# Float32 probabilities with 128-wide values in differential attention, a column-packed condition product, and moved splits in the MLP

## The chip, the cores and the metric

One core of a Trainium2 chip runs the whole program. The metric is the device time of one execution in microseconds, lower is better. The engines are TensorE (PE, with its weight loads listed apart as PEld), VectorE (DVE), ScalarE (ACT), GpSimd (POOL) and SyncE (SP), which issues most of the DMAs. Each engine works through its own instructions in order and waits on semaphores.

## The reference

Two blocks follow each other on 1024 tokens of width 1024. The first block has two layers with 256 context tokens; each layer has three kinds of attention, and the first kind, differential attention, is the one that the change touches. The second block mixes three other heads and ends in an MLP with a squared ReLU. Cut to what matters here:

```python
# the condition: shift, scale and gate from silu(c) @ w_ada + b_ada, for c and for c_ctx
# first kind of attention: 4 heads, two maps of width 32, values of width 64
def diff_attend(q, k, v, lam):
    s = jnp.einsum('bqhmd,bkhmd->bhmqk', q, k).astype(jnp.float32) * (q.shape[-1] ** -0.5)
    p = jax.nn.softmax(s, axis=-1)
    a = (p[:, :, 0] - lam * p[:, :, 1]).astype(v.dtype)
    return jnp.einsum('bhqk,bkhd->bqhd', a, v)

# the end of the second block: width 1024 -> 4096 -> 1024
h = h + jnp.square(jax.nn.relu(hn @ w_up[l])) @ w_down[l]
```

## The kernel before

**Precision.** Most large products are float32 products in three passes: each operand is split into a high part in the reduced float32 type (a ScalarE copy) and a low part (a subtraction on VectorE or GpSimd), and `mm3` (lines 73 to 75) adds high times high, high times low and low times high. A few products take plain float32 operands. A plain float32 product appears in the trace as two TensorE instructions, one in the reduced type as one.

**The condition.** `ada_first` (lines 101 to 127) multiplies `silu(c)` (two columns: c and c_ctx) with the first 2048 columns of `w_ada`, 8 pieces of 1 MB through four buffers, 4 products of 512 columns for each piece, all plain float32. Two rows of the result are transposed by 16 small transposes (line 126). `modulate` makes from them the shift and gain that the first tile of the first projection needs.

**Attention.** `attend_kind` treats a kind as a row of units, one unit for each head and 128 queries (and one for both context tiles, in layer 0). The order of the work on every engine is written out by hand in `cfgs[...]["order"]`: S scores, M row minimum, E exponential, C combination of the two maps, T transposes, K copies out of PSUM, J pieces of the product with v, O1 to O4 output. The kinds run in the order A, C, B in both layers. For kind A the probabilities of one unit are 128 x 1280, transposed in three groups of 4, 4 and 2 blocks. `whole=4` means that the first four blocks of 128 keys are split: ScalarE copies the group out of PSUM (`pf`, line 728), GpSimd makes the high part (`th`, line 729) and the low part (`tl`, line 730). The other six blocks stay float32 (`tf`, line 724). `products` then works for each pair of units: four blocks give two products each (high and low) against `v`, which holds the two parts of the values beside each other, 128 wide; six blocks give one float32 product each against `vf`, the sum of both parts, 64 wide, made by GpSimd once for each head (line 425) after the load of v. `cuts` says at which products the six J pieces begin. `load_head` issues the loads of the next head on GpSimd's queue, four for k and q and one for v, when the current head is at its third unit.

**The MLP.** Both MLP products use a seven-product scheme over 2 x 2 blocks, with numbers p from 1 to 7. `mlp_up` runs 16 column groups g; `prep` makes the parts `wh` and `wl` of a weight (lines 1589, 1571), two steps ahead; `wl` goes to VectorE for the first six steps and for p of 1 or 2, otherwise to GpSimd. `startup` makes the split right-hand factors B[1] to B[7] during the first steps; the low part of B[4] is made on GpSimd, and only when it is done is the space of `hraw` free, on which the tiles of `late` lie. `mlp_down` runs 4 slices s with seven products each; its own `prep` splits a weight tile `w` (VectorE) and an activation tile `u` (GpSimd), two halves each (lines 1742 and 1710). The first of these preparations stands behind the last step of `mlp_up`. In the last slice the finished sums are combined (line 1711) and stored.

## Time and profile before

| | |
|---|---|
| median of 3 runs | 3794.61 us (3781.96 to 3800.78) |
| the profiled execution | 3782.26 us |
| its span, first to last instruction | 3780.5 us |
| TensorE busy | 3441.1 us (91%) |
| VectorE busy | 2397.9 us (63%) |
| ScalarE busy | 1763.5 us (47%) |
| GpSimd busy | 1594.2 us (42%) |
| mean granted TensorE clock | 0.957 of full speed |

The stages lie in the span as follows: the condition from 0 to 43 us, the projection of layer 0 to 495 us, kind A to about 700, C to about 890, B to about 1085, the output product to 1160; in layer 1 the projection to about 1620, kind A to about 1830, C to 1995, B to 2215, the output product to 2300; then the second block with its projections, its scans from about 2700, its output product, the first MLP product from 3127 to 3451 and the second to the end.

A busy share is an average over these stages. In a table of stretches the columns are: the stretch, its length, for each engine its busy time and number of instructions, the granted clock as a share of full speed, the busy share of the DMA engines and GB/s. In a list of instructions in order of time the columns are: start, duration, engine, line, operation, what it writes and reads, how many were merged, and in brackets the idle time of the engine before it and what ended it. Records of TensorE overlap (the end contains the way through the array), so its pace is read from start to start.

### The profile page before, as it was taken

What the parts mean: (1) busy time and instruction counts of PE and PEld (TensorE: products, weight loads), DVE (VectorE), ACT (ScalarE), POOL (GpSimd) and SP (SyncE); (2) the same over time, 40 slices, a digit from 0 to 9 for tenths busy, and PEclk for the clock granted to TensorE, in tenths of its full rate; (3) what the DMA queues carried; (4) which work ended last, traced back from release to release, by engine and by line L of the source; (5) the groups of instructions that cost most, each with busy time, mean ns of one, the idle gap of its engine ahead of it and who ended that gap; (6) DMA issues with size and microseconds to landing.
All of it is one profiled execution on the core that took longest, in us unless ns stands there. A gap on an engine that the chain in (4) does not pass through costs nothing. (4 is left out here: it accounts for less than half of the span.)

```text
span 3780.5 us, 50490 instructions
## 1 busy us (share of the span) xinstructions
PE 3441.1 (91%) x17986; PEld 2760.7 (73%) x17986; DVE 2397.9 (63%) x4543; ACT 1763.5 (47%) x3667; POOL 1594.2 (42%) x1692
## 2 busy tenths in 40 slices
PE   8989978888989899978898989999799898999999
PEld 5767755677877788756677767887677677887887
DVE  5666469777774635559776664422688637555778
ACT  4212257677851422247667733321476525554432
POOL 1146434325760235535426741112455415554556
PEclk9999989999999999979999989999899999999999
DMA  7564662662223434592661124121311223545542
GB/s 264 194 182 131 152 111 48 95 115 51 43 79 131 166 126 143 140 113 45 108 100 42 23 104 162 60 64 51 89 40 37 76 84 126 164 153 188 194 144 106
DMA packets 281359, 420.20 MB, mean 111 GB/s; under 512 B 49586, under 2 KB 179186, under 8 KB 276370
## 3 DMA queue, kind: packets, MB, share of 16 engines
q1 hardware_dynamic: 204244, 336.07, 27.4%
q0 software_dynamic: 76864, 80.90, 14.1%
q8 instruction: 142, 2.33, 0.3%
q14 instruction: 109, 0.89, 0.1%
HBM read 289.30 MB, written 127.48 MB: 110 GB/s over the span
## 5 line engine op out<-in xcount | busy, mean ns | idle before, releaser
L74 PE MATMUL mm<-wlo,hh 128*128 128x512 f32 (+2 forms) x1400 | 546.0, 390 | 18.1 <-POOL wlo L94 11.7
L73 PE MATMUL mm<-whi,hh 128*128 128x512 f32 (+2 forms) x1400 | 553.5, 396 | 8.8 <-ACT hh L68 5.3
L75 PE MATMUL mm<-whi,hl 128*128 128x512 f32 (+2 forms) x1400 | 546.7, 391 | 2.1 <-DVE hl L69 2.1
L698 PE MATMUL T<-ident,p 128*128 128x128 f32 x2288 | 382.4, 288 | 37.6 <-DVE y L777 9.5
L94 POOL TENSOR_TENSOR wlo<-wraw,whi 128x512 fp32r<-128x512 f32 (+1 forms) x108 | 164.7, 1532 | 477.6 <-ACT whi L92 402.7
L698 PEld LDWEIGHTS T<-ident,p 128*128 128x128 f32 x2288 | 267.6, 146 | 108.4 <-issue 24.2
L473 PE MATMUL s<-k,q 128*128 128x256 f32 (+2 forms) x904 | 251.0, 384 | 77.9 <-ACT p L476 43.5
L74 PEld LDWEIGHTS mm<-wlo,hh 128*128 128x128 f32 (+1 forms) x1400 | 264.5, 189 | 76.5 <-POOL wlo L94 16.7
L73 PEld LDWEIGHTS mm<-whi,hh 128*128 128x128 f32 (+1 forms) x1400 | 264.5, 189 | 62.6 <-ACT hh L68 6.8
L75 PEld LDWEIGHTS mm<-whi,hl 128*128 128x128 f32 (+1 forms) x1400 | 264.1, 189 | 61.7 <-DVE hl L69 6.0
L730 POOL TENSOR_TENSOR tl<-pf,th 128x512 fp32r<-128x512 f32 (+1 forms) x256 | 288.5, 1133 | 13.4
L729 POOL TENSOR_SCALAR th<-pf 128x512 fp32r<-128x512 f32 (+1 forms) x256 | 153.8, 605 | 267.6 <-ACT pf L728 267.1
L473 PEld LDWEIGHTS s<-k,q 128*128 128x128 f32 x904 | 149.1, 200 | 122.9 <-ACT p L476 66.1
L626 DVE TENSOR_REDUCE mm<-s 128x1 f32<-128x1280 f32 x128 | 188.8, 1477 | 63.8 <-PE s L473 63.5
L69 DVE TENSOR_TENSOR tl<-T,th 128x512 fp32r<-128x512 f32 (+2 forms) x336 | 178.4, 551 | 46.9 <-ACT th L68 44.7
L1710 POOL TENSOR_TENSOR f<-u,f 128x1024 fp32r<-128x1024 f32 x54 | 153.8, 2872 | 121.3 <-issue 106.6
L476 ACT ACTIVATE p<-s,mm 128x1280 f32<-128x1280 f32 (+1 forms) x156 | 184.1, 1183 | 35.8 <-DVE mm L626 32.9
L74 PE MATMUL D<-f,f 128*128 128x512 f32 x448 | 177.2, 396 | 6.0 <-DVE f L1710 5.9
L73 PE MATMUL D<-f,f 128*128 128x512 f32 x448 | 176.7, 395 | 5.6 <-ACT f L1742 5.6
L236 ACT ACTIVATE q_sq<-mm 128x512 f32<-128x512 f32 (+1 forms) x76 | 41.1, 541 | 299.2 <-DVE qk_ss L242 119.1
L73 PE MATMUL mm<-whi,yh 128*128 128x512 f32 x416 | 171.6, 413 | 9.0 <-ACT yh L68 7.3
L94 DVE TENSOR_TENSOR wlo<-wraw,whi 128x512 fp32r<-128x512 f32 (+1 forms) x108 | 102.7, 957 | 120.2 <-ACT whi L92 115.4
(453 smaller groups left out, 9112.3 us busy)
## 6 DMA issues: line engine op xcount, KB each, us to landing
wraw<-in_w_in_dram SPq DMA_DIRECT2D x72, 512.0 KB, 4.2
u<-ud SPq DMA_DIRECT2D x27, 1024.0 KB, 4.8
w<-in_w_adat_dram SPq DMA_DIRECT2D x64, 256.0 KB, 3.3
upraw<-in_w_up_dram SPq DMA_DIRECT2D x32, 512.0 KB, 4.5
ud<-d SPq DMA_DIRECT2D x64, 256.0 KB, 2.6
wq<-in_w_down_dram SPq DMA_DIRECT2D x16, 1024.0 KB, 7.4
v<-vd POOLq DMA_DIRECT2D x24, 640.0 KB, 11.2
q<-qd POOLq DMA_DIRECT2D x24, 640.0 KB, 20.5
```

What stands on the lines that cost most here:

```text
L69: self.nc.vector.tensor_tensor(out=lo, in0=src, in1=hi, op=ALU.subtract)
L73: nc.tensor.matmul(ps, lh, rh, start=first, stop=False)
L74: nc.tensor.matmul(ps, lh, rl, start=False, stop=False)
L75: nc.tensor.matmul(ps, ll, rh, start=False, stop=last)
L94: e.tensor_tensor(out=lo[:, k, :], in0=raw[:, k, :], in1=hi[:, k, :], op=ALU.subtract)
L473: self.nc.tensor.matmul(out, q[:, tcol : tcol + P], ks, start=i == 0, stop=i == len(qs) - 1)
L476: self.nc.scalar.activation(out, in_, AF.Exp, bias=nm, scale=-1.0, accum_out=acc)
L626: nc.vector.tensor_reduce(out=mm[:, m, 0:1], in_=s[:, :SK], axis=AX.X, op=ALU.min)
L698: nc.tensor.transpose(pt[:, i, :], p[:, (4 * g + i) * P : (4 * g + i + 1) * P], self.ident)
L729: nc.gpsimd.tensor_scalar(out=h_, in0=pf, scalar1=1.0, scalar2=0.0, op0=ALU.mult, op1=ALU.add)
L730: nc.gpsimd.tensor_tensor(out=l_, in0=pf, in1=h_, op=ALU.subtract)
L1710: sub = lambda e, o, x, y: e.tensor_tensor(out=o, in0=x, in1=y, op=ALU.subtract)
```

## The change

It has four parts.

1. **Kind A.** `whole` goes from 4 to 0: all ten blocks of the transposed probabilities are copied out of PSUM by ScalarE as float32, no block is split, and GpSimd has neither `th` nor `tl` to make in this kind. `vf` becomes 128 wide, with zeros in columns 64 to 127 (a GpSimd memset for each head), and each pair of units has ten float32 products with 128-wide weights. The cuts of the six J pieces move with it.
2. **The condition.** `silu(c)` is padded to 32 columns, and the four products of a piece write to four groups of 32 columns of the array and 32 rows of PSUM each. The bias row becomes 128 x 2048 with zeros below the first two rows. The 16 transposes become 16 float32 products with a selector that adds the four groups.
3. **First MLP product.** `wl` goes to VectorE for the first twelve steps rather than six. The last column group has the order of the others.
4. **From the first to the second MLP product, and the last slice.** The tiles of B[1] and B[2] are kept and serve as one of two sets of split tiles in `mlp_down` (before: eight rotating tiles). The split of the first pair of factors (`down_split`) is put into `mlp_up`, behind step p = 7 of the last group. In the last slice the additions into A(6) (at p = 1) and A(5) (at p = 7) go from VectorE to GpSimd, those into A(6) one step later.

```diff
@@ ada_first
-            sc = self.t(p, [P, KO, 2], tag="silu_c")
-            nc.sync.dma_start(sc, I["cc"])
...
+            sc = self.t(p, [P, KO, 32], tag="silu_c")
+            nc.vector.memset(sc, 0.0)
+            nc.sync.dma_start(sc[:, :, 0:2], I["cc"])
...
+            row = self.t(p, [P, 4 * 512], tag="row")
+            nc.vector.memset(row, 0.0)
+            nc.sync.dma_start(row[0:2, :], I["b_ada"].broadcast_to([2, 4 * 512]))
+            sel = self.t(p, [P, 2], tag="sel")
...
-                        nc.tensor.matmul(pr, sc[:, kk, :], w[:, k, :], start=kk == 0, stop=kk == KO - 1)
+                        nc.tensor.matmul(pr[32 * k : 32 * k + 32, :], sc[:, kk, :], w[:, k, :], start=hf == 0, stop=hf == 1, tile_position=(0, 32 * k), skip_group_check=True)
...
-                nc.tensor.transpose(pt[:, j, :], row[:, j * P : (j + 1) * P], self.ident[0:2, 0:2])
+                nc.tensor.matmul(pt[:, j, :], row[:, j * P : (j + 1) * P], sel, start=True, stop=True)
@@ load_v
-            vf = self.t(pool, [P, NTA, 64], tag="vf")
+            vf = self.t(pool, [P, NTA, P], tag="vf")
             f = v.bitcast(F32)
-            nc.gpsimd.tensor_tensor(out=vf, in0=f[:, :, 0:64], in1=f[:, :, 64:128], op=ALU.add)
+            nc.gpsimd.memset(vf[:, :, 64:128], 0.0)
+            nc.gpsimd.tensor_tensor(out=vf[:, :, 0:64], in0=f[:, :, 0:64], in1=f[:, :, 64:128], op=ALU.add)
@@ cfgs
-        "A": dict(whole=4, poolg=((0,),), dsplit=SK, pp=6, apl=3, psT=2, psO=0, cuts=(0, 6, 9, 10, 11, 13, 14), order=(
+        "A": dict(whole=0, poolg=((),), dsplit=SK, pp=6, apl=3, psT=2, psO=0, cuts=(0, 2, 4, 6, 7, 9, 10), order=(
@@ products
-                if s >= whole:
-                    ops.append((64, c, w, d["vf"][:, b, :], tf[:, s - whole, c : c + w]))
+                if tf is not None and s >= whole:
+                    ops.append((P, c, w, d["vf"][:, b, :], tf[:, s - whole, c : c + w]))
@@ mlp_first, mlp_up
-        self.bp = self.bs.enter_context(tc.tile_pool(name="mb1", bufs=1, side="right", reuse_waits="tile"))
+        self.bp = self.b1s.enter_context(tc.tile_pool(name="mb1", bufs=1, side="right", reuse_waits="tile"))
-            sub(nc.vector if n < 6 or p in (1, 2) else nc.gpsimd, lo, src, hi)
+            sub(nc.vector if n < 12 or p in (1, 2) else nc.gpsimd, lo, src, hi)
-        steps = first + [(g, p) for g in range(NG) for p in ((1, 6, 2, 5, 7, 3, 4) if g < NG - 1 else (1, 2, 6, 5, 7, 3, 4)) if (g, p) not in first]
+        steps = first + [(g, p) for g in range(NG) for p in (1, 6, 2, 5, 7, 3, 4) if (g, p) not in first]
+            if (g, p) == (NG - 1, 7):
+                self.down_split(self.first[0], self.first[2], [*B[1], *B[2]])
+    def down_split(self, w, u, dst):
+        nc = self.nc
+        wh, wl, uh, ul = dst
+        for k in (0, 2):
+            c = slice(k, k + 2)
+            for hi, lo, x, e in ((wh, wl, w, nc.vector), (uh, ul, u, nc.gpsimd)):
+                nc.scalar.copy(hi[:, c, :], x[:, c, :])
+                e.tensor_tensor(out=lo[:, c, :], in0=x[:, c, :], in1=hi[:, c, :], op=ALU.subtract)
@@ mlp_down
-            hl = E("dhl", 8, side="right")
+            hl = E("dhl", 1, side="right")
+            sets = [[*self.B[1], *self.B[2]], [self.t(hl, [P, 4, 512], F32R, tag=f"f{i}") for i in range(4)]]
...
+                fac[s, p] = sets[(7 * s + order.index(p)) % 2]
+                if (s, p) != (0, 1):
+                    self.down_split(w, u, fac[s, p])
...
-                        add(v, A(6), A(6), a)
                     elif p == 2:
+                        add(gp, A(6), A(6), A(1))
...
-                        add(v, A(5), A(5), a)
+                        add(gp, A(5), A(5), a)
```

## Rows read from the trace of the kernel before

**Rows 1.** The page, part 1: busy time, share of the span, instructions of each engine.
```profile
PE 3441.1 (91%) x17986; PEld 2760.7 (73%) x17986; DVE 2397.9 (63%) x4543; ACT 1763.5 (47%) x3667; POOL 1594.2 (42%) x1692
```
**Rows 2.** Table of stretches: layer 1's kind A, then two of the MLP.
```profile
1720.00:1800.00 80.00, 72.36 (x407) 51.13 (x405) 78.17 (x117) 65.03 (x123) 44.77 (x40) 1.00 0.30 52
...
3440.00:3470.00 30.00, 22.52 (x80) 17.06 (x79) 9.87 (x9) 11.96 (x17) 16.13 (x8) 0.77 0.68 244
3470.00:3700.00 230.00, 230.00 (x1016) 190.50 (x1015) 178.55 (x140) 90.51 (x100) 120.16 (x42) 1.00 0.48 171
```
**Rows 3.** In order of time, the condition up to the first large product.
```profile
7.53 30.30 PE L121 MATMUL pr<-w,silu_c 128*2 128x512 f32 x64 [7.53 <-DMA w<-in_w_ada_dram]
...
39.84 0.17 DVE L136 COPY sh<-pr 128x16 f32<-128x16 f32 x1 [1.29 <-PE pr L126]
...
42.86 0.50 PE L73 MATMUL mm<-whi,hh 128*128 128x512 f32 x1 [1.22 <-ACT hh L68]
```
**Rows 4.** Table of stretches inside the condition.
```profile
5.00:10.00 5.00, 2.47 (x3) 0.37 (x4) 0.00 (x0) 0.00 (x0) 0.00 (x0) 1.00 1.01 428
```
**Rows 5.** In order of time, second block's scans: TensorE products of other shapes.
```profile
2713.33 0.72 PE L1243 MATMUL M<-qx 64*128 64x128 f32 x8
...
2730.19 1.03 PE L1438 MATMUL A<-state,cv 128*128 128x256 f32 x4
2731.05 1.19 PE L1443 MATMUL A<-xdt,dec 128*128 128x64 f32 x9
```
**Rows 6.** In order of time, layer 1's kind A: products with v on TensorE.
```profile
1727.34 0.28 PE L762 MATMUL T<-tl,v 128*128 128x256 f32 x1
1727.55 1.51 PE L762 MATMUL T<-tf,vf 128*64 128x256 f32 x6
1728.99 0.73 PE L473 MATMUL s<-k,q 128*128 128x512 f32 x2
...
1736.64 0.28 PE L762 MATMUL T<-tl,v 128*128 128x256 f32 x1
1736.76 0.28 PE L762 MATMUL T<-th,v 128*128 128x256 f32 x1
```
**Rows 7.** Groups of instructions on VectorE in 1720 to 1800 us (count; busy us, mean ns; idle).
```profile
L626 DVE TENSOR_REDUCE mm<-s 128x1 f32<-128x1280 f32 x31 | 45.7, 1476 | 1.5 <-PE s L473 1.5
L685 DVE SCALAR_TENSOR_TENSOR p<-p,cf,p 128x640 f32<-128x640 f32 x31 | 31.9, 1045 | 0.0
```
**Rows 8.** In order of time, layer 0's kind A: one combination with GpSimd idle.
```profile
647.46 0.89 DVE L685 SCALAR_TENSOR_TENSOR p<-p,cf,p 128x640 f32<-128x640 f32 x1
```
**Rows 9.** In order of time, layer 1's kind A, at the second head's load.
```profile
1671.05 1.53 POOL L425 TENSOR_TENSOR vf<-v 128x640 f32<-128x640 f32 x1 [20.39 <-DMA v<-vd]
...
1674.44 0.58 PE L762 MATMUL T<-th,v 128*128 128x256 f32 x1 [9.66 <-POOL th L729]
```
**Rows 10.** In order of time, the first steps of the first MLP product.
```profile
3146.42 8.41 POOL L1571 TENSOR_TENSOR wl<-s,wh 128x512 fp32r<-128x512 f32 x2 [15.01 <-ACT wh L1589]
...
3153.66 0.80 PE L1609 MATMUL d<-b7h,wl 128*128 128x512 f32 x1 [6.53 <-POOL wl L1571]
...
3156.49 5.39 POOL L1555 TENSOR_TENSOR b4l<-hraw,b4h 128x512 fp32r<-128x512 f32 x4
...
3162.66 0.79 PE L1609 MATMUL c<-b3h,wh 128*128 128x512 f32 x1 [4.63 <-DVE U L1572]
```
**Rows 11.** From first to second MLP product, and groups of the second's splits.
```profile
3456.83 1.22 PE L73 MATMUL D<-f,f 128*128 128x512 f32 x2 [5.57 <-ACT f L1742]
```
**Rows 12.** Groups of instructions over the span: splits and additions of the second product.
```profile
L1710 POOL TENSOR_TENSOR f<-u,f 128x1024 fp32r<-128x1024 f32 x54 | 153.8, 2872 | 121.3 <-issue 106.6
...
L1711 DVE TENSOR_TENSOR a<-a,a 128x512 f32<-128x512 f32 x20 | 23.0, 1181 | 0.2
...
L1711 POOL TENSOR_TENSOR a<-a,a 128x512 f32<-128x512 f32 x12 | 19.5, 1653 | 3.0 <-DVE a L1711 3.0
```
**Rows 13.** In order of time, the last slice.
```profile
3751.94 0.80 PE L74 MATMUL D<-f,f 128*128 128x512 f32 x1 [5.11 <-DVE f L1710]
```

More of the change, by code (lines that the diff above doesn't have):

```diff
@@ L108, in ada_first @@
             psum = es.enter_context(tc.tile_pool(name="adaps", bufs=2, space=PSUM))
-            sc = self.t(p, [P, KO, 2], tag="silu_c")
-            nc.sync.dma_start(sc, I["cc"])
-            nc.scalar.activation(sc, sc, AF.Silu)
-            row = self.t(p, [2, 4 * 512], tag="row")
-            nc.sync.dma_start(row, I["b_ada"].broadcast_to([2, 4 * 512]))
+            sc = self.t(p, [P, KO, 32], tag="silu_c")
+            nc.vector.memset(sc, 0.0)
+            nc.sync.dma_start(sc[:, :, 0:2], I["cc"])
+            nc.scalar.activation(sc[:, :, 0:2], sc[:, :, 0:2], AF.Silu)
+            row = self.t(p, [P, 4 * 512], tag="row")
+            nc.vector.memset(row, 0.0)
+            nc.sync.dma_start(row[0:2, :], I["b_ada"].broadcast_to([2, 4 * 512]))
+            sel = self.t(p, [P, 2], tag="sel")
+            nc.vector.tensor_tensor(out=sel, in0=self.ident[:, 0:2], in1=self.ident[:, 32:34], op=ALU.add)
+            for g in (2, 3):
+                nc.vector.tensor_tensor(out=sel, in0=sel, in1=self.ident[:, 32 * g : 32 * g + 2], op=ALU.add)
             for ch in range(4):
-                pr = self.t(psum, [P, 512], tag="pr")[0:2, :]
+                pr = self.t(psum, [P, 512], tag="pr")
                 for hf in range(2):
@@ L709, in keep @@
                 R = lambda tag, k, dt=F32R, **kw: self.t(self.tp, [P, k, 256], dt, tag=tag, **kw)
-                tt[h, pr] = (R("ch", 2, bufs=1), R("cl", 2, bufs=1), None) if j == 2 else (R("th", whole), R("tl", whole), R("tf", NTA - whole, F32) if whole < NTA else None)
+                tt[h, pr] = (R("ch", 2, bufs=1), R("cl", 2, bufs=1), None) if j == 2 else (R("th", whole) if whole else None, R("tl", whole) if whole else None, R("tf", NTA - whole, F32) if whole < NTA else None)
             th, tl, tf = tt[h, pr]
@@ L1543, in mlp_first @@
         tc = self.tc
-        self.bs = ExitStack()
-        self.bp = self.bs.enter_context(tc.tile_pool(name="mb1", bufs=1, side="right", reuse_waits="tile"))
+        self.bs, self.b1s = ExitStack(), ExitStack()
+        self.bp = self.b1s.enter_context(tc.tile_pool(name="mb1", bufs=1, side="right", reuse_waits="tile"))
         self.B = {}
@@ L1738, in prep @@
                 w, u = b(*src), us.pop((s, p))
-                wh, wl, uh, ul = [self.t(hl, [P, 4, 512], F32R, tag="f") for _ in range(4)]
-                def split(hi, lo, x, e):
-                    nc.scalar.copy(hi, x)
-                    sub(e, lo, x, hi)
-                for k in (0, 2):
-                    c = slice(k, k + 2)
-                    split(uh[:, c, :], ul[:, c, :], u[:, c, :], gp)
-                    split(wh[:, c, :], wl[:, c, :], w[:, c, :], v)
-                fac[s, p] = wh, wl, uh, ul
+                fac[s, p] = sets[(7 * s + order.index(p)) % 2]
+                if (s, p) != (0, 1):
+                    self.down_split(w, u, fac[s, p])
             def put(t, half, ch, c):
@@ L1848, in block2 @@
         self.mlp_down(out)
+        self.b1s.close()
 def rope_table(d):
```

## The prediction

> **What bounds the kernel now.** The page comes first: TensorE is busy 91% of the span [rows 1], so in most stages only a TensorE that stands still or works less is worth anything. Then the stages one by one, in the table of stretches. In the middle of the second product of the MLP it is busy for all 230 us, 1016 matmuls, 0.226 us each, at the full clock of 2.4 GHz [rows 2]; that is the pace to compare with. Three places differ from that. In kind A of layer 1 VectorE is busy 78.2 of 80 us and TensorE 72.4 [rows 2]: here VectorE is the bound, a unit takes 80 us over 15.5 (31 row minima are two to a unit [rows 7]), 5.16 us. In the condition TensorE works without a break from 7.5 to 37.8 us on products with two columns of weights [rows 3]. And at both ends of the MLP's products it waits for splits of VectorE, ScalarE and GpSimd [rows 10, 11, 13]. The change touches just these places. All the rest (projections, kinds B and C, output products, scans) is left as it is.
>
> The profiled execution took 3782.26 us with a span of 3780.5; the median of the runs is 3794.61, 12 us more. The savings below are read from that one execution and taken off the median, since that is what a later median is compared with.
>
> **1. The condition: 8 us less (between 2.5 more and 11 less).** Now 64 instructions take 30.30 us, 0.47 each [rows 3]. Afterwards four products go to four groups of columns. Whether such groups run beside each other this trace doesn't show. The nearest row is the scans' products on 64 rows, which alternate between two groups of rows: 8 instructions in 0.72 us, 0.064 from start to start ((0.72 - 0.27 of passage) / 7), where the 64-column product, of fewer columns, takes 0.115 ((1.19 - 0.27) / 8) [rows 5]. So the second instruction of one product runs beside the first of the next, and I take half: a piece of 8 instructions lasts 4 x 0.47 = 1.9 us. That is less than its transfer: 1.05 MB at the 428 GB/s of the first stretch [rows 4] is 2.45 us, so the 8 pieces land from 5 to about 24.6, and the DMA becomes the bound. The two new memsets stand on VectorE, and SP's load of the bias row, with all pieces queued behind it, waits for the larger one: 2048 columns, at most the 1.48 us of a 1280-column reduction [rows 7] scaled, 2.4; I take 1, as nothing is read. End of the last piece: 24.6 + 1 + 1.9 = 27.5. The selector products are 32 instructions instead of 16; at 0.115 [rows 5] 24 of them run while VectorE adds the last row (2.8 us), 8 after (0.9): 31.2. From the first use of that result to the first large product it is 42.86 - 39.84 = 3.0 us [rows 3], which gives 34.2 instead of 42.86, 8.7 less. The loads of x and of the first weights now queue behind the pieces and cost some of it: 8. If the groups don't overlap at all, TensorE still ends at 37.8 or 1 us later, and 16 more short instructions add 1.5: 2.5 more. The upper end lets all four groups run together and the memset vanish.
>
> **2. Kind A, the stall at the second head: 10 us less (0 to 13).** In layer 1 GpSimd sits 20.39 us before `vf` because v of the next head is still on its way, and TensorE waits 9.66 us for a `th` queued behind it [rows 9]. Afterwards `th` isn't made by GpSimd at all, and what the products need comes from ScalarE. GpSimd waits as before, now with only the memset, `vf` and the next head's loads queued behind, which are needed a head later. The lower end is that the next head's k and q are themselves only just there.
>
> **3. Kind A, the steady part: 12 us less (10 more to 21 less).** Off TensorE first, for a pair of units. Now: 8 reduced products at 0.12 from start to start, 0.96; 12 float32 instructions at 0.216, 2.59; and the change of weight width around each of the two groups: entry 0.21 instead of 0.12, and 1.44 for six instead of 6 x 0.216 = 1.30, so 2 x 0.23 = 0.46 [rows 6]. Sum 4.01. Afterwards: 20 instructions. A 128-wide float32 product of 256 columns is in the trace: four in 1.03 us, (1.03 - 0.38) / 3 = 0.216 [rows 5], as much as the 64-wide one, and the next product follows 0.86 after the first of the four, so with no extra for leaving. 20 x 0.216 = 4.32, plus 0.31 a pair, 0.16 a unit. Over 64 units of queries (4 heads, 8 tiles, 2 layers) that is 10 us of TensorE. On ScalarE three copies stay three copies of the same sizes, nothing. On GpSimd `th` and `tl` vanish. What this gives VectorE: the combination of the two maps takes 1.045 on average here [rows 7] and 0.89 where GpSimd stands idle [rows 8]; twice a unit that is 0.31, or 0.33 with the wait of a small operation between. So VectorE falls from 5.04 busy a unit (78.17 / 15.5) to 4.7, TensorE rises from 4.67 (72.36 / 15.5) to 4.83. Both then lie below 5.16, but close together, and a unit with two engines so full won't reach 4.83. I take 0.2 of the possible 0.33 a unit, and 60 units, as some stand in the start and the stall: 12. If all of the relief comes through, 0.33 x 64 = 21; if none, TensorE's 10 come on top.
>
> **4. Start of the first MLP product: 5 us less (0 to 10).** TensorE waits 6.53 us for a `wl` of GpSimd, and later 4.63 for VectorE's U [rows 10]. The two first `wl` take GpSimd 8.41 us together, and then b4l begins at 3156.49 and runs 5.39 [rows 10]; U lies in the space that only b4l sets free. With the `wl` on VectorE, GpSimd can begin b4l some 5 us earlier, as its input was there. VectorE takes on six subtractions in the first twelve steps, about 0.6 to 0.7 each, of which three stand ahead of U; b4's input, too, hangs on VectorE. So the first wait goes and the second moves up: both don't add, as the second is then later for TensorE by what the first no longer costs. 5 is the shift of U.
>
> **5. From the first to the second product: 6 us less (0 to 11.9).** In 3440 to 3470 80 matmuls at 0.226 would be 18.1 of 30 us [rows 2]: 11.9 lost, 5.57 of it as one wait for a split by ScalarE [rows 11], the rest in waits behind it and at a mean granted clock of 0.77. With the split issued two steps (5.4 us of TensorE) earlier, ScalarE's four copies stand ahead of, or between, the squares of the last two steps, and the additions and stores of these come later on VectorE, GpSimd and SP. GpSimd then needs 2 x 2.87 [rows 12] for the low halves of u, which end some 4 us after TensorE wants them, with TensorE's work between; and SP's loads of the next weights stand behind the last store of the first product, so they don't come much earlier. I keep 5 to 6 of the 11.9 as lost.
>
> **6. The last slice: 3 us less (5 more to 7.5 less).** TensorE waits 5.11 us for a split by VectorE [rows 13] and starts again at the half clock, some 2.4 more. Eight additions of 1.18, 9.4 us, leave VectorE; on GpSimd they take 1.65 each, 13.2 [rows 12], beside the splits of u that the next product waits for (5.7 of the 10.9 us that a product of 48 matmuls lasts). GpSimd gets full there, so I count less than half of the 7.5. At TensorE's end nothing changes.
>
> The Trainium skill, SBUF — State Buffer, section "SBUF: two separate sides", says that GpSimd and a VectorE instruction with two SBUF inputs share a port pair by an exclusive lock, and that whoever comes second waits for the whole of the other. In part 3 the rows have the sign of it (0.89 against 1.045); for part 6 it speaks against the change, and there it is the rival R3.
>
> **Sum.** 8 + 10 + 12 + 5 + 6 + 3 = 44; 3794.6 - 44 = 3751 us.
>
> **The rivals.**
> - R1, TensorE binds kind A: the relief of VectorE finds no use and the 0.16 a unit appear in full. For it: TensorE already has 72.4 of 80 us [rows 2] and one order for all. Against it: VectorE is the fuller one. Part 3 turns from -12 to +10: 3773 us.
> - R2, the column groups run one after the other, so the change of the condition doesn't do what it says. For it: the trace has no product with several column groups. Against it: the row groups overlap [rows 5]. Part 1 turns from -8 to +2.5: 3761 us.
> - R3, VectorE and GpSimd exclude each other in the last slice: moved additions lengthen the sum of both by 8 x (1.65 - 1.18) = 3.8 us [rows 12], and the late split is GpSimd's instead of VectorE's. Part 6 turns from -3 to +4: 3758 us. That is what the skill's rule above would give.
> - R4, slower than before: the 128-wide float32 weights can't be loaded beside the running product when transposes and scores stand between. A load that is exposed for 0.14 us, a quarter more than the 0.115 of the shortest pace in [rows 5], at 20 x 32 instructions is 90 us of TensorE, 1.4 a unit; it decides from about 0.33 a unit, where TensorE passes VectorE's 5.16. A unit would be 4.83 + 1.4 = 6.2, 1.07 over now, 64 x 1.07 = 68 us more where I have 12 less; with the other parts 32 less: 3831 us. Against it: four such products follow at 0.216 without a gap [rows 5].
>
> **How the numbers follow.** The forecast 3751 has a chance of 0.64, with its own range of 3730 to 3770; R1 0.14, R2 0.08, R3 0.08, R4 0.03, and 0.03 for what I don't see. The range 3724 to 3778 takes in R1 to R3 and most of what the bounds allow when they add up by chance, not all in one direction. A difference of 0.5%, 19 us, is about what a measurement of this kernel can tell from no change. Faster by more than that means below 3775.6: the forecast (0.62), R2 and R3, half of R1 (0.08): 0.86. Within it: the rest of the forecast and of R1, and a part of the unseen: 0.10. Slower: R4 and the rest: 0.04.
>
> **What the profile afterwards would show.** The first large product at 34 us, not 43 (38 or later is R2), with the stretch from 10 to 25 us at some 420 GB/s. In kind A: units of about 4.95 us, combinations at 0.89, float32 products of L762 at 0.216 from start to start with none at 64 columns (above that is R4), no wait of TensorE near 10 us; if VectorE falls to 4.7 a unit and the unit stays at 5.2, it is R1. In the MLP: the wait for U about 5 us earlier, the first D product some 5 us nearer to the last product of the first stage, and in the last slice a wait shorter than 5.11, or one that names GpSimd's split (R3). The forecast is wrong above all if kind A gives nothing, or if a moved split is late for something that isn't late now.

## The result and the profile after

The changed kernel takes 3743.35 us (median of 4 runs, 3736.88 to 3754.78), the kernel before, beside it, 3790.53 (3781.96 to 3800.78): 0.9879 of it, 95% interval 0.9852 to 0.9905, some 46 us less. Run again beside the experiments it came to 0.9886 (0.9858 to 0.9914). The forecast was 3751. The profiled executions differ by the same amount, a span of 3735.1 against 3780.5, and since most stages repeat to a few tenths the difference can be split by stage. A stage lasts from the first product of its kind to the first of the next; kind A ends at its last copy of an output (20 in layer 0, 16 in layer 1). An output belongs to a pair of units. By this count kind C of the kernel before ends at 871.7 and 1976.2 us, some 20 us earlier than the rough division further up has it.

| stage | before | after | difference | forecast |
|---|---|---|---|---|
| start to kind A of layer 0 (condition, projection) | 494.4 | 491.6 | -2.9 | -8 |
| kind A, layer 0 and layer 1 | 220.1, 205.3 | 218.8, 192.9 | -13.8 | -22 |
| kind C, layer 0 and layer 1 | 157.1, 146.8 | 144.1, 139.5 | -20.3 | 0 |
| first MLP product, first 112 instructions | 42.9 | 40.4 | -2.5 | -5 |
| first MLP product, the rest | 280.2 | 279.0 | -1.2 | 0 |
| last of the first to third of the second MLP product | 34.1 | 32.6 | -1.6 | -6 |
| last two products of the last slice and the end | 34.1 | 35.2 | +1.1 | -3 |
| all that the change leaves alone | 2165.4 | 2161.2 | -4.2 | 0 |

The sum is right, the shares aren't: kind C gave 20 us that nobody had forecast, and every forecast term is too large. The last row is a net of larger ones, though no code of these stages changed: the second block's scans are 7.0 us longer and the stretch ahead of them 7.4 shorter.

The page, part 1 (compare [rows 1]):

```profile
PE 3421.2 (92%) x18002; PEld 2796.0 (75%) x18002; DVE 2377.1 (64%) x4546; ACT 1762.6 (47%) x3665; POOL 1458.8 (39%) x1574
```

Kind A's steady part in layer 1, 16 units, as a table of stretches (compare [rows 2]):

```profile
1680.00:1766.70 86.70, 76.92 (x432) 64.06 (x432) 79.00 (x121) 68.83 (x130) 8.24 (x10) 1.00 0.46 70
```

A unit takes 86.7 / 16 = 5.42 us, with TensorE busy 4.81 of it and VectorE 4.94. Before, the same units took 5.28. So the steady part has become 0.14 us a unit slower, although VectorE's combination fell just as [rows 8] promised. In this stretch, the group of the combination, and then the waits (who for whom, us in total, times, longest):

```profile
L694 DVE SCALAR_TENSOR_TENSOR p<-p,cf,p 128x640 f32<-128x640 f32 x32 | 27.5, 881 | 0.4
```
```profile
ACT tf L733 <- PE T L707: 15.3, 16, 1.9
...
PE s L482 <- ACT p L485: 9.8, 16, 0.8
...
DVE r L689 <- ACT p L485: 6.4, 4, 1.6
```

No engine is full; each waits for another a little. What answers to [rows 9] is gone: between the first and the fourth output of layer 1's kind A there are 33.6 us instead of 48.9.

In order of time, the condition (compare [rows 3]), and below it three stretches of the changed kernel:

```profile
18.18 1.06 PE L128 MATMUL pr<-w,silu_c 128*32 128x512 f32 x8 [0.80 <-DVE row L130]
20.58 1.93 PE L128 MATMUL pr<-w,silu_c 128*32 128x512 f32 x8 [1.33 <-DMA w<-in_w_ada_dram]
...
25.02 5.28 PE L133 MATMUL pr<-sel,row 128*128 128x2 f32 x24
...
30.23 1.93 PE L128 MATMUL pr<-w,silu_c 128*32 128x512 f32 x8
...
37.95 0.79 PE L73 MATMUL mm<-whi,hh 128*128 128x512 f32 x1 [1.30 <-ACT hh L68]
```
```profile
10.00:25.00 15.00, 10.50 (x48) 1.22 (x48) 2.07 (x3) 0.00 (x0) 0.00 (x0) 0.85 1.01 421
25.00:35.00 10.00, 9.18 (x46) 7.42 (x43) 0.81 (x3) 4.18 (x5) 3.25 (x4) 0.50 0.74 295
35.00:45.00 10.00, 8.32 (x28) 6.01 (x26) 7.67 (x22) 6.36 (x9) 1.25 (x3) 0.53 0.54 160
```

The eight instructions of the piece at 18.18 last 1.06 us at the full clock, where one alone took 0.47 [rows 3]: all four column groups run at once. The pieces behind it take 1.93 at a granted clock of 0.50. Those ahead of it take 1.8 to 1.9 too; the trace's record of the clock begins only at 17.1 us, and the column counts the time ahead of that as 1.00. The transfer has become the bound, at 421 GB/s. But 24 selector products stand ahead of the last piece, and from 20.5 to 44.4 us the granted clock is half (1.2 GHz), where before it was full from 40 us on.

The MLP: its start, the way to the second product, and the last slice (compare [rows 10], [rows 11] and [rows 13]); each fence is in order of time.

```profile
3110.54 7.67 POOL L1564 TENSOR_TENSOR b4l<-hraw,b4h 128x512 fp32r<-128x512 f32 x4 [19.99 <-ACT b4h L1563]
...
3114.18 0.79 PE L1618 MATMUL b<-b6h,wh 128*128 128x512 f32 x1 [4.76 <-ACT wh L1598]
...
3118.99 0.80 PE L1618 MATMUL c<-b3h,wh 128*128 128x512 f32 x1 [4.02 <-DVE U L1581]
```
```profile
3414.51 0.32 SPq L1607 DMA_DIRECT2D ud<-d  x1
3416.87 0.32 SPq L1744 DMA_DIRECT2D u<-ud  x1
3417.28 9.64 SPq L1740 DMA_DIRECT2D wq<-in_w_down_dram  x6
...
3424.43 1.99 ACT L1715 CAST f<-wq 128x1024 fp32r<-128x1024 f32 x2 [5.44 <-DMA wq<-in_w_down_dram]
...
3425.53 2.07 PE L73 MATMUL D<-f,f 128*128 128x512 f32 x4 [7.93 <-ACT f L1715]
```
```profile
3703.36 0.69 PE L75 MATMUL D<-b1h,b2l 128*128 128x512 f32 x1 [1.71 <-POOL b2l L1716]
...
3709.57 0.50 PE L75 MATMUL D<-b1h,b2l 128*128 128x512 f32 x1 [2.64 <-POOL b2l L1716]
```

### The profile page after: what moved, and what is told of

It is laid out like the page before. It is cut to its first block, busy times and chain, and to the rows that moved or that the text cites. A ratio compares the mean times of both kernels' runs of the same rounds, so it can differ in the third digit from the quotient of the medians.

```text
span 3735.1 us, 50394 instructions
## 1 busy us (share of the span) xinstructions
PE 3421.2 (92%) x18002; PEld 2796.0 (75%) x18002; DVE 2377.1 (64%) x4546; ACT 1762.6 (47%) x3665; POOL 1458.8 (39%) x1574
## 4 chain that ended last, share of the span: by engine, by line
PE 43%; DVE 6%; issue 5%; ACT 5%; POOL 4%; DMA 4%; SPq 0%; POOLq 0%; ACTq 0%; DVEq 0%
PE mm L75 4%; PE mm L74 4%; PE mm L73 4%; PE D L73 3%; PE D L75 3%; PE D L74 2%; PE c L1618 2%; PE d L1618 2%; PE a L1618 2%; PE T L707 2%; ACT p L485 2%; PE T L771 2%; DMA q<-qd 1%; PE O L771 1%; PE b L1618 1%
## 5 line engine op out<-in xcount | busy, mean ns | idle before, releaser
L707 PE MATMUL T<-ident,p 128*128 128x128 f32 x2288 | 370.6, 285 | 30.6 <-DVE tl L69 7.3
L707 PEld LDWEIGHTS T<-ident,p 128*128 128x128 f32 x2288 | 266.3, 144 | 89.2 <-issue 14.3
L739 POOL TENSOR_TENSOR tl<-pf,th 128x512 fp32r<-128x512 f32 x192 | 193.1, 1014 | 9.3
L68 ACT CAST th<-T 128x512 fp32r<-128x512 f32 (+2 forms) x336 | 156.2, 483 | 59.2 <-PE T L707 55.6
L74 PE MATMUL mm<-wlo,yh 128*128 128x512 f32 x416 | 169.1, 407 | 4.4 <-POOL wlo L94 4.4
L75 PE MATMUL mm<-whi,yl 128*128 128x512 f32 x416 | 165.0, 404 | 8.6 <-DVE yl L69 8.3
L92 ACT CAST whi<-wraw 128x1024 fp32r<-128x1024 f32 (+1 forms) x108 | 110.6, 1033 | 125.3 <-DMA wraw<-in_w_in_dram 80.8
```

The source lines that it names most:

```text
L68: self.nc.scalar.copy(hi, src)
L74: nc.tensor.matmul(ps, lh, rl, start=False, stop=False)
L75: nc.tensor.matmul(ps, ll, rh, start=False, stop=last)
L707: nc.tensor.transpose(pt[:, i, :], p[:, (4 * g + i) * P : (4 * g + i + 1) * P], self.ident)
L739: nc.gpsimd.tensor_tensor(out=l_, in0=pf, in1=h_, op=ALU.subtract)
```

## The experiments

**Kind A's part alone, and everything but it.** Two kernels: `a_only` is the kernel before with the edits of `cfgs`, `load_v`, `keep` and `products`; `a_undone` is the changed kernel without them.

> The kernel before with kind A's part alone (no split, values 128 wide, cuts moved). Between the two traces the stretch from the first score of kind A to the first score of kind B, which holds kinds A and C, is 14.3 us shorter in layer 0 (377.2 to 362.9) and 19.8 in layer 1 (352.1 to 332.3). If that is all of this part's doing, the time is 34 us less than before, 0.991 of it, and the stages of the MLP and the condition stand as before. If the gain of kinds A and C needs the other parts (a shifted start, another place in memory), less than 20.

> The changed kernel with kind A as before. If the parts add up, 10 to 13 us less than before, 0.997 of it: 3 to 5 from the condition, 2.5 from the start of the MLP, 1.6 from its middle, nothing or a loss of 1 in the last slice, the rest by chance. The wait of TensorE near 10 us at layer 1's second head comes back, and kind C's wait for its q with it.

Measured: 0.9928 of before (0.9911 to 0.9945), 27 us less, for kind A's part; 0.9988 (0.9975 to 1.0002), 5 us less, for the rest. In the trace of `a_only` kinds A and C are 17.1 us shorter in layer 0 (14.3 in the changed kernel); in layer 1 6.5 instead of 19.8, because a wait appears there that the changed kernel's trace doesn't show (below, j_queue). `a_undone` has the wait at the second head again (49.4 us from the first to the fourth output) and kind C at 157.0 and 149.0. So the gain of kinds A and C is this part's own, and the three other parts together are worth about as little as the measurement can tell.

**GpSimd given its splits back.** The first four blocks are split as before, out of `tf`, and nobody reads the parts:

```diff
                         nc.scalar.copy(f_, src)
+                        if g == 0:
+                            nc.gpsimd.tensor_scalar(out=th[:, :, c], in0=f_, ...)
+                            nc.gpsimd.tensor_tensor(out=tl[:, :, c], in0=f_, in1=th[:, :, c], op=ALU.subtract)
```

> The changed kernel in which GpSimd again makes a high and a low part of the first four blocks of each unit of kind A, as it did before, out of the copy that ScalarE makes; nobody reads them. Theory G, the gain comes from GpSimd's free queue (no product waits behind its loads any more, and the loads of the next head and of kind C are issued earlier): since no product waits for GpSimd here, layer 1's stall of 10 us stays away, but kind C's loads are issued late again and 5 to 8 us a layer are lost at kind C's start; a unit of the steady part stays within 0.1 of 5.42. Theory V, the gain comes from VectorE's faster combinations (0.88 instead of 1.045): they are back at 1.0 or more, a unit becomes 5.7 or longer, and 10 us a layer are lost inside kind A.

Measured: 1.0026 of before (1.0007 to 1.0045): all of the gain is lost and more. Both theories held, each in its place. Kind C is back at 150.9 and 150.8 us (theory G), and a unit of kind A takes 5.90 us (theory V; G had said 5.5 at most), with the combination at 0.956 and the small product ahead of it at 0.45 instead of 0.21, together 0.39 us of VectorE a unit. The stall stays away, as G had it (38.7 us from the first to the fourth output). So a free GpSimd does two things: it lets kind C's loads go out in time, and it keeps the unit short. Without it the float32 form is 0.6 us a unit slower than the kernel before, instead of 0.14. That VectorE's 0.39 is what makes the unit 0.48 longer here is likely, but was not tried by itself.

**64 wide instead of 128.**

```diff
-                    ops.append((P, c, w, d["vf"][:, b, :], tf[:, s - whole, c : c + w]))
+                    m = 64 if ops else P
+                    ops.append((m, c, w, d["vf"][:, b, 0:m], tf[:, s - whole, c : c + w]))
```

> The changed kernel with nine of the ten float32 products of a pair 64 wide, as six were before; only the first stays 128 wide, to clear all rows. Theory W, leaving and entering the 64 wide form costs 0.23 us for each group: six groups a pair, 1.4 us, 0.7 a unit, and TensorE goes from 4.81 to 5.5 of a unit, above the 5.42 that it takes now: 5.6 to 6.0 a unit, 10 to 35 us more in both layers. Rival: the width doesn't matter, because the scores wait for ScalarE anyway (0.6 us a unit): 5.4 as now.

Measured: 6.04 us a unit, and kinds A and C together 12.0 and 24.4 us longer than changed. Theory W holds, just above its upper end. In layer 1 some 8 of the 24.4 are something else: at the second head TensorE waits 4.78 us for q, the lower end that the prediction's part 2 had named, and the pair there takes 20.2 us instead of 11.9. In order of time (layer 1):

```profile
1727.79 1.17 PE L772 MATMUL T<-tf,vf 128*128 128x256 f32 x4
1728.89 0.66 PE L707 MATMUL T<-ident,p 128*128 128x128 f32 x4
1729.47 1.51 PE L772 MATMUL T<-tf,vf 128*64 128x256 f32 x6
```

From the start of the four products to the transposes 1.10 us pass, where the same four take 0.86 in the changed kernel (1724.28 to 1725.14 there). That the change of width costs some 0.23 for entry and exit was read rightly from [rows 6].

**What sets the unit.** In three heads one thing each is taken away:

```diff
+                    if kind == "A" and h == 1 and units[n][2] < 2 and x in (1, 3, 5, 8):
+                        continue
...
+            if h == 2 and j < 2:
+                w //= 2
...
-                nc.vector.tensor_reduce(out=mm[:, m, 0:1], in_=s[:, :SK], axis=AX.X, op=ALU.min)
+                nc.vector.tensor_reduce(out=mm[:, m, 0:1], in_=s[:, : SK // 2 if h == 3 else SK], axis=AX.X, op=ALU.min)
```

> The changed kernel, with one thing taken out of kind A in each of three heads (in both layers; layer 1 is read), so that these heads' results are not the reference's. First head: nothing. Second head: 4 of the 10 float32 products of a pair are left out, 1.73 us of TensorE a pair, 0.86 a unit. Third head: the combination of the two maps takes half of the columns, some 0.8 us of VectorE a unit. Fourth head: the row minimum reads half of the columns, some 1.4 us of VectorE a unit, and each score's way to its exponential gets 0.7 shorter. A unit takes 5.42 us with TensorE busy 4.81 and VectorE 4.8 of them. Theory L, the round of scores, row minimum, exponential and free score buffer (two buffers) sets the unit: 5.3 to 5.5 in the second and third heads, 4.7 or less in the fourth. Theory P, TensorE sets it: 4.5 to 4.7 in the second head, 5.4 in the others. Theory E, VectorE sets it: 5.4 in the second head, 4.6 in the third, 4.0 in the fourth.

The table of stretches, 7 units of the second head, 6 of the third, 4 of the fourth:

```profile
1681.26:1715.17 33.91, 28.82 (x164) 22.38 (x162) 32.57 (x54) 29.11 (x55) 5.22 (x6) 1.00 0.58 68
1719.75:1753.28 33.53, 29.23 (x161) 23.47 (x160) 27.22 (x49) 26.48 (x51) 4.16 (x5) 1.00 0.32 76
1753.28:1775.75 22.47, 19.71 (x109) 16.08 (x108) 14.95 (x30) 17.15 (x32) 0.98 (x1) 1.00 0.21 40
```

4.84, 5.59 and 5.62 us a unit. Only less work for TensorE makes a unit shorter; less for VectorE, on or off the way from score to exponential, does not (it is even 0.2 longer; the runs don't show why). Theory P is nearest, though its 4.5 to 4.7 wasn't reached: 0.69 us less of TensorE (28.82 / 7 = 4.12) brought 0.58. Theories L and E fall.

**The MLP as before.** In the changed kernel `n < 12` goes back to `n < 6`, the last group to its own order, the first `down_split` behind the last step, the additions to VectorE.

> The changed kernel with the MLP as before (six steps of low parts on VectorE, first split of the second product behind the last step of the first, additions on VectorE in the last slice). Read at the products of TensorE: the first 112 of the first MLP product take 42.9 us again (40.4 changed), the way from the last product of the first to the third of the second 34.1 (32.6), the next to last product of the last slice 18.8 (20.4), and what follows it 15.2 (14.8). If the parts of the MLP act where they stand, that is 2.5 + 1.6 - 1.6 + 0.5 = 3.0 us more than the changed kernel, and kinds A and C and the condition stand as changed.

Measured, against the changed kernel: the start 42.6 (+2.2) and the rest of the first product 280.3 (+1.2), as expected. The way to the third product 32.0 (-0.6), not 34.1. That doesn't show the earlier split to be worth nothing, since this kernel has it too: its first copy starts 17.0 us ahead of the last product of the first matrix, in the changed kernel 15.7 ahead, and before 3.4 us behind it. The place of the line in the code doesn't decide when the split runs; the tiles of B[1] and B[2], in which it now lands, are a candidate, not tried by itself. The last two products and the end 33.3 (-1.9): the moved additions are a loss, as rival R3 had it, if a smaller one than its 3.8 us. In sum it is about 1 us more than the changed kernel, not 3.0.

**Three things mended.** The selector products of a quarter are issued behind the next quarter's pieces; the second product of the second matrix takes the weight that is already there, and the next weights stand ahead of the activations; the additions go back to VectorE.

```diff
+                if ch:
+                    columns(ch - 1)
+            columns(3)
...
+            self.down_split(q[0, 1, 0], None, sets[1])
...
-            for b, c in ((1, 0), (0, 0), (0, 1), (1, 1)):
+            for b, c in ((0, 0), (0, 1), (1, 1), (1, 0)):
...
+                        add(v, A(6), A(6), a)
-                        add(gp, A(6), A(6), A(1))
```

> The changed kernel with three things mended. The selector products of a quarter stand behind the next quarter's pieces instead of 24 of them ahead of the last piece: the first large product at 33 to 34 us instead of 37.95; if the granted clock or the transfer is what holds it, 36 or later. The second product of the second MLP matrix takes the weight that already lies in memory instead of loading it again, and the third's weights stand ahead of the activations on SP's queue: the wait of 7.9 us goes, and from the last product of the first stage to the third of the second it is 22 to 25 us instead of 32.6; if GpSimd's splits are what is late, 29 or more. The additions of the last slice are back on VectorE: its next to last product takes 18.8 instead of 20.4, the end 15.2 instead of 14.8. Together 12 to 15 us less than the changed kernel.

> The changed kernel once more, beside the others on the same chip. Its stages repeat within 1 us except those whose length is decided by when transfers land or by the granted clock: the scans of the second block (327 to 345 us so far in six traces of the same code) and kind A's start in layer 1. Against the kernel before 0.986 to 0.991.

Measured: the first large product at 34.8 us, in the three kernels built on it at 33.2 to 34.7; in the seven traces with the changed condition it stands at 35.1 to 38.0. The way to the third product 22.05 us, exactly two products of 10.9 and nothing between; of the 10.5 us won, 2.8 come back at the fourth product. The last two products and the end 33.7. From the last product of the first matrix to the end it is 319.65 us, where the changed kernel takes 328.9: 9.2 less, and within 0.6 of that in the traces of j_queue, j_wide4 and j_wide2 as well. The whole, however, is 0.9885 of before (0.9839 to 0.9931), beside 0.9886 (0.9858 to 0.9914) for the changed kernel (the run `again`) on the same chip: a stage that neither touches took 354 us in its profile instead of 334. The stretch of the second block's scans, in before, changed and joined:

```profile
2682.21:3009.09 326.88, 288.89 (x1958) 221.66 (x1958) 254.95 (x466) 213.02 (x632) 167.71 (x231) 0.92 0.19 49
```
```profile
2635.78:2969.62 333.84, 297.09 (x1957) 227.94 (x1958) 254.49 (x466) 213.66 (x632) 168.14 (x231) 0.89 0.19 48
```
```profile
2639.10:2993.40 354.30, 318.11 (x1957) 243.36 (x1958) 255.81 (x466) 215.08 (x632) 168.00 (x231) 0.82 0.17 45
```

The same instructions, all other engines equally busy, and only the granted clock differs: 0.92, 0.89, 0.82. So a part of 9 us must be read from its stage; the total can't show it in four runs. How far a stage repeats, the trace of `again` shows: kind A and the four rows of the MLP within 0.5 us of the changed kernel's first trace, as expected, but kind C 1.6 more and 1.2 less, and the first large product 2.9 earlier.

The condition's gain, by contrast, does not arrive. In the seven traces with the changed condition the first score of kind A stands at 491.6 to 495.1 us (mean 493.4), in three with the old one at 494.4 to 494.8 (mean 494.6). With the selectors in place it is 490.1 to 492.0 in four traces (mean 491.0).

**GpSimd's queue.** Is it the products or the queue? `b_queue` is the kernel before with its products untouched:

```diff
+            if kind == "A" and n < N and units[n][0] and units[n][1:] == (0, 1):
+                with self.tc.issue_after(self.mark):
+                    self.sum_v(self.data[kind, units[n][0]])
+            if kind == "A" and n == N // 2 + 2:
+                with self.tc.issue_after(self.mark):
+                    self.load_head(l, "C", 0)
```

> The kernel before, its arithmetic untouched, with GpSimd's queue in another order in kind A: the sum of the values' halves for heads two to four stands behind low parts of the head before, not right behind the load of v, and the loads of kind C's first head are issued in the middle of kind A. Theory G, what the change gained in kinds A and C is GpSimd's queue (products wait for a high part that stands behind a wait for v; kind C's loads are issued late): in layer 1 the fourth output of kind A comes 34 to 38 us after the first instead of 48.9, kind C in layer 1 takes 140 instead of 147, in layer 0 145 instead of 157, and the whole is 25 to 32 us less than before, nearly all of the 34 that kind A's part gave, with no product changed. Theory F, it is the float32 products themselves (no high parts to wait for, a freer VectorE): within 8 us of before.

Measured: the stall goes. From the first to the fourth output of layer 1's kind A 36.8 us pass instead of 48.9. The sum of the halves and the longest wait of TensorE for GpSimd there (order of time; waits):

```profile
1701.42 1.54 POOL L405 TENSOR_TENSOR vf<-v 128x640 f32<-128x640 f32 x1
```
```profile
PE T L775 <- POOL tl L742: 0.3, 1, 0.3
```

No 20 us of waiting ahead of it [rows 9], and 0.3 instead of 9.66. So that stall was the queue, not the split. But kind A of layer 1 as a whole is no shorter (205.4 us, before 205.3): its first output comes 4.9 us later, with ScalarE waiting 7.78 for a store, and a later pair, right behind the loads of kind C's first head, takes 16.1 instead of 10.5. The order that removes one stall makes others. And the whole is 1.006 of before (1.0039 to 1.008), which neither theory had: kind A of layer 0 takes 241.0 instead of 220.1 (the wait of ScalarE shown below for j_queue, here 26.35 us), and kind C stays at 156.8 and 148.4. The second half of theory G was wrong in its detail: it is not the loads of kind C's first head that matter. What does: in kind C TensorE waits for q of the next heads, and how long depends on whether GpSimd had splits to make in kind A. All 14 traces:

| | kind C, layer 0 | kind C, layer 1 | of it waiting for q |
|---|---|---|---|
| GpSimd splits in kind A (before, a_undone, a_gp, b_queue, j_wide4, j_wide2) | 150.1 to 157.1 | 146.8 to 154.7 | 14.2 to 18.3; 15.6 to 21.7 |
| it doesn't (changed, again, joined, j_queue, a_only, m_undone, a_heads, a_64) | 141.3 to 146.1 | 138.3 to 140.4 | 6.9 to 11.1; 6.9 to 9.7 |

The waits of TensorE in layer 1's kind C, before and changed:

```profile
PE s L473 <- DMA q<-qd: 15.6, 3, 10.2
```
```profile
PE s L482 <- DMA q<-qd: 8.7, 2, 5.5
```

The loads stand in GpSimd's queue. Before, those of kind C's second and third heads were issued 34 and 6 us ahead of kind A's last output in layer 1, among the last splits; afterwards 62 and 21 us ahead. In layer 0 it is 42 and 11 us before, and the third head's 24 afterwards. The longest of the waits is the third head's: before, the q in question is issued 4.8 us ahead of kind A's last output and lands 25.4 us later, and TensorE waits 10.2 us for it; afterwards it is issued 18.4 us ahead, lands 1.6 us after that output, and nothing waits. In a_gp, issued 5.4 us ahead, it is waited for again, 6.8 us. In layer 0 the same wait of 7.8 us goes. All waits for q together fall by 7 us in each layer, which is nearly all that kind C gains in layer 1 (7.3), and half in layer 0 (13.0). That the earlier issue is what shortens kind C fits every trace; it was not tried alone.

**The same order in the mended kernel, and other splits.** Three kernels on top of joined: the queue alone; four blocks split as before, but the six others 128 wide; two blocks split.

> The kernel of the run joined, with the loads of kind C's first head issued in the middle of kind A instead of at its start. In three of eight traces with kind A as changed, ScalarE waits 13 to 16 us at the start of layer 1's kind A for the last store of the gate, which shares its memory with the new float32 tiles and lands as late as 40 us, beside those loads. If the loads delay the store: it lands within 15 us of the first score and the first output comes 36 to 38 us after it, never 50. If the store is late for another reason, 50 remains possible. The unit stays at 5.42, kind C as in joined; 0 to 6 us less than joined in the median.

> The run j_queue with four blocks split again as before, but the six float32 blocks with values 128 wide: a pair of units then needs 8 x 0.12 + 12 x 0.216 = 3.55 us of TensorE instead of 4.32 (changed) or 4.01 (before, 64 wide), as no group enters or leaves another width. GpSimd makes the high and low parts again, so VectorE's combinations are back at 1.05. Theory P, TensorE sets the unit (taking 0.86 a unit off it made the unit 0.6 shorter): 5.0 to 5.2 a unit. Theory E, VectorE with 5.04 of it sets it: 5.2 to 5.3. Either way 5 to 13 us a layer less than 5.42. Against it: GpSimd's queue stands in the way again, as in a_gp, where a unit took 5.90: 5.5 or more.

> The same with two blocks split instead of four: 4 x 0.12 + 16 x 0.216 = 3.94 us of TensorE a pair, half of GpSimd's high and low parts, one more copy of ScalarE a unit. Between the two: TensorE 4.64 a unit, VectorE some 4.9. Theory P 5.1 to 5.3 a unit, theory E 5.0 to 5.2; if GpSimd's work is what lengthens the unit, 5.5.

Measured: 0.9937 (0.9918 to 0.9956), 0.9975 (0.9957 to 0.9992), 0.9984 (0.9968 to 1.0000) of before. All are slower than changed. With splits on GpSimd a unit took 5.72 (four) and 5.56 (two) in the mean of the same 16 units, not 5.0 to 5.3, as the last case of each expectation had it. But in j_wide4 the mean holds two slow pairs: of the nine between the fourth and the thirteenth output of layer 1 they take 8.1 and 7.2 us a unit, and the seven others 4.90 to 5.34, where theory P had them. The first of the two stands where the order of j_queue puts the loads and masks of kind C's first head: GpSimd works on them from 1727.8 to 1736.4 us, and a `pf` finished at 1730.1 gets its high part only from 1736.6. So the 0.39 us of TensorE that this split takes off a unit do shorten it and are lost again in GpSimd's queue; this split without that order was not tried. The order also cost 24 us at the start of layer 0's kind A in j_queue, and 17 in each of the other two. ScalarE, in order of time, j_queue and before:

```profile
519.51 0.25 ACT L182 COPY gr<-T 16x128 f32<-16x128 f32 x1 [28.98 <-DMA gate<-gr]
```
```profile
502.14 0.25 ACT L169 COPY gr<-T 16x128 f32<-16x128 f32 x1 [7.37 <-DMA gate<-gr]
```

ScalarE waits 29 us for SyncE's store of 8 KB. GpSimd had issued the five loads of the next head at that moment (before, they follow from 504.60 on, behind its work for kind C's first head), and they need as long (DMA issues of j_queue between 489 and 493 us: KB each, median us to landing):

```profile
k<-ka POOLq DMA_DIRECT2D x2, 640.0 KB, 29.1
...
v<-vd POOLq DMA_DIRECT2D x1, 640.0 KB, 29.7
```

The same shows in layer 1 of a_only, m_undone and a_heads, where the first float32 tiles lie on memory that the last store of the gate still reads. In a_only:

```profile
1647.91 1.07 ACT L725 COPY tf<-T 128x512 f32<-128x512 f32 x2 [15.57 <-DMA gd<-sg]
```
```profile
k<-kd POOLq DMA_DIRECT2D x1, 640.0 KB, 40.5
...
gd<-sg SPq DMA_DIRECT2D x1, 256.0 KB, 39.4
```

The expectation that the loads of kind C make it fell: in j_queue, which doesn't issue them there, it is still 6.8 us, in j_wide2 12.0. All told it appears in 7 of 14 traces, with 6.1 to 15.6 us, b_queue with its tiles as before among them. In layer 0 it is 24.9 to 29.0 us in all four kernels with the new order and 5.9 to 9.9 in the ten others. Which of GpSimd's transfers holds the store, and why in layer 1 only in some executions, is open.

## Why the prediction came out

- **Sum.** 44 us forecast, 46 measured. It is right because errors cancel: the six terms gave 21 (2.9 + 13.8 + 2.5 + 1.2 + 1.6 - 1.1), 23 less than forecast, and kind C 20 that it hadn't; 4 came from stages that the change leaves alone. That the number came out is luck.
- **1, the condition (8 forecast; 4.9 at the first large product, about 1 at kind A).** Of the rivals R2 was wrong: the groups overlap fully. The transfer is the bound, as worked out, and the 1.9 us of a piece was met, though for another reason (full overlap; behind 20.5 us at a granted clock of 0.50, ahead of 17.1 without a record of it). Two steps failed. "24 of them run while VectorE adds the last row (2.8 us)": they stand ahead of the last piece, and take 5.28 us, 0.22 each and not 0.115. And the step behind: TensorE, no longer busy without a break, comes to the projection at a granted clock of 0.53 instead of 1.00. The 25th product of the projection starts at 50.2 us, before at 50.6: the gain is gone after 24 products. Of the 4.5 us given back, 1.6 are order alone: eight transposes that stood ahead of the first product now stand behind the sixth. With the selectors in place (joined and what is built on it) 3.6 of it arrive in the mean, not 8.
- **2, the stall (10 forecast; 12 to 15).** Right, in place and cause: b_queue removes the wait at this place by the queue alone, if with no gain for the whole of kind A. The size was low because the pairs behind it had been slow too: 13.7, 11.3 and 11.8 us against 10.5 further on.
- **3, the steady part (12 less forecast; 3 more).** Behind the fourth output, kind A takes 271.1 us in both layers together instead of 267.9. The base was misread first: "80 us over 15.5" gives 5.16 a unit, but the 31 row minima of that stretch start from 1720.1 to 1799.7, 30 steps of 2.65, so 5.30 a unit, with 5.18 of VectorE and 4.80 of TensorE in it. The combination came down as worked out (0.881 against 0.89), VectorE to 4.94 a unit (4.7 forecast), TensorE stands at 4.81 (4.83 forecast). By the Trainium skill, SBUF — State Buffer, section "SBUF: two separate sides", the combination should be slowed by GpSimd's work; a_gp agrees, where it takes 0.956 with GpSimd at work again. The step that failed is "I take 0.2 of the possible 0.33 a unit". Being the fuller engine did not make VectorE the bound: in a_heads its relief does nothing and TensorE's does nearly all. R1's mechanism, at a chance of 0.14, is nearest to what happened here, with 0.14 a unit instead of 0.16.
- **Kind C (0 forecast; 20).** The failed step is in part 2: "only the memset, `vf` and the next head's loads queued behind, which are needed a head later". It stopped at kind A's last head. GpSimd carries the loads of the next kind as well, and there they were late.
- **4, the start of the MLP (5 forecast; 2.5).** `b4l` does begin 5.1 us earlier (23.7 after the first product instead of 28.8), as worked out, but takes 7.67 instead of 5.39: the first of its four subtractions lasts 4.01 instead of 1.73, beside VectorE's (busy until 3113.4, two of the moved ones among them), the other three 1.26 each in both. The term that was mis-sized is the duration of this subtraction; that VectorE's work is the reason was not tried by itself. Nor does the first wait go: 6.53 for GpSimd's `wl` becomes 4.76 for a `wh` of ScalarE, whose input VectorE makes behind the moved subtractions.
- **5, the transition (6 forecast; 1.6).** The earlier split does its part: the first product of the second matrix follows 0.2 us after the last of the first, before 6.0. The text itself said that the next weights "stand behind the last store", and then counted only 5 to 6 us as lost. They decide it: the wait of 5.57 in front of the first product became one of 7.93 in front of the second, at the same half clock behind. Joined, which takes that load out of the way, gains 10.5.
- **6, the last slice (3 less forecast; 1.1 more).** R3: the late split is GpSimd's (1.71 and 2.64 us), as it named; m_undone and joined win the loss back.
- **R4** did not occur: float32 products 128 wide show the pace of [rows 5], and it is the 64-wide form that costs.

## What to carry to other kernels

When work is taken off an engine that also issues loads, follow its queue to the end, into the next stage: what stood behind that work there may be worth more than the work. A moved split or load gains only if the next thing on the same chain is ready; ask which load the following product waits for before taking away the wait in front. And an engine that is the fullest is not therefore the bound in an order written by hand: take a little work off each engine in turn and see which one moves the period. And an edit that is taken back in the code is taken back only if the trace shows the work at its old place.

## What the runs showed of the hardware

- Four float32 products of 32 columns each on four column groups run fully together: 8 instructions in 1.06 us, where one alone took 0.47.
- A small store by SyncE that is issued among GpSimd's loads can land about when they do: ScalarE waited 29 us for one of 8 KB, and one of 256 KB took 39.4, beside loads that took 29.1 and 40.5. The Trainium skill, DMA: Bandwidth & Descriptors, "Queues, rings and completion order", has each DMA engine alternate between queues by packets, and says that the increment that tells of a landing comes only after every earlier write of that engine, across its queues. The second would have the sign of these rows; no run here shows what holds the store.
- The granted clock in one stage of unchanged code ranged from 0.82 to 0.92 between executions, and its time from 354 to 327 us. No other stretch of unchanged code varies as much in the 14 traces.
- A GpSimd subtraction of 128 x 512 float32 columns took 4.01 us beside VectorE's subtractions, and 1.26 with VectorE standing still. That one causes the other was not tried by itself.
